# A streaming-encoder block in three-pass fp32: the second query block's mixed heads are loaded earlier, and two output-projection products take the last chunk last

## The chip, the cores and the metric

The kernel runs on one core of one Trainium2 chip. The metric is the device time of one execution in microseconds. An execution is somewhat longer than the span that the profiler shows from its first to its last instruction.

## The reference

One transformer-like layer over 2048 positions of width 1024, in float32:

```python
h = rms_norm(x, norm_mix_g)
z = h @ w_in                                   # columns: u_a, v_a (512 each), q, k, v (512 each), 8 forget logits
out_a = u_a * (masked W_s @ LN(v_a) + b)       # 8 gated-MLP heads, blocks of 128 positions
c = cumsum(log_sigmoid(f_logit))
s = q @ k.T / 8 + c[t] - c[s], causal          # 8 forgetting-attention heads of size 64
out_b = softmax(s) @ v
x = x + concat(out_a, out_b) @ w_out           # the output projection, 1024 x 1024
a = rms_norm(x, norm_ffn_g) @ w_up             # 1024 -> 2 x 2816
a = causal depthwise conv of width 3 over positions
x = x + (silu(g) * val) @ w_down
out = rms_norm(x, norm_final_g)
```

## The kernel before

**Arithmetic.** A float32 product is made of three passes: each operand is split into a high and a low part, and hi·hi, hi·lo and lo·hi are added in PSUM. `mm3` (L209) issues them: 8 chunks of 128 along the contracted dimension, three products each, 24 of 128x512 per output tile. `whi`/`wlo` are parts of weights (GpSimd makes `whi` at L152 from the loaded `raw`, VectorE `wlo`), `thi`/`tlo` parts of activations.

**Stages.** The 2048 rows are two halves of 1024, each half two blocks of 512 (`tb` = 0 to 3). The program first makes norms, `w_in` and the gated-MLP heads for all rows. `c_half(0)` is the output projection of the first half, `d_half` its up-projection with convolution, then the second half and the down-projection follow.

**Attention runs alongside.** It is a generator with many small steps. Each product of the dense stages calls `tick`, and after a certain number of products one step of attention is written into the program, with a priority that puts it some way ahead of the dense work around it. `need(tb)` writes steps until the heads of block `tb` are done. The flag `self.ready` lets the heads of the second half (`tb` of 2 and 3) begin. For each pair of heads, `b_max` looks for the row maxima (key products L829, VectorE reductions L832), `b_mix` computes scores (L877, L881), exponentials (L886), the high part `ph` and low part `pl` (L891, L892), their sum (L894) and the product with V (L865, L866). At the end of a pair both heads are put into one tile `op` (L906, L907), the reciprocal sums are turned by four transposes into `s` and multiplied in (L923). The pair is then split by `split_sb` (L203, L204) and written to DRAM, to `mixh` and `mixl`, from where the output projection loads it.

**The last pair of the first half** (`h` = 7, `tb` = 1) does not take the way through DRAM: it is split straight into chunk 7 of the projection's operand. `load_mix(1, given)` therefore loads only chunks 0 to 6, in pieces of two chunks. An operand has two tiles for each of hi and lo: one with chunks 0 to 3 and one with chunks 4 to 7.

**The output projection** (`c_half`) takes the two blocks `b` in turn, in each two column halves of `w_out` (in the order 0, 1 and then 1, 0, so that the weights of column half 1 are used twice in a row), in each four output tiles `t` of 128 rows. Such a tile is a PSUM sum "mm", of which there are two banks. VectorE adds the row of x to it (L971), and after the second column half the row is written to DRAM (`rows`), scaled by its norm (ScalarE L180, GpSimd L976, tile `ar`), and later transposed in pieces ("dn", L190) and split (L199, L200) for the up-projection.

**What sets the order.** The written order, the priorities and a scheduler that simulates the engines give the order on each engine; within an engine instructions run in that order. All loads and stores are issued by SyncE (SP) from line L102, in order. `issue_after(i)` keeps a load from being issued ahead of instruction `i`.

Of the kernel before, what the change touches and what calls it, by code (L numbers as in the profile page):

```python
# [8 lines left out]
F32 = mybir.dt.float32  # L9
# [9 lines left out]
P = 128  # L19
S = 2048  # L20
D = 1024
KC = D // P
# [3 lines left out]
TB = 512  # L26
# [7 lines left out]
AHEAD_B, AHEAD_W = 100, 2000  # L34
# [20 lines left out]
def f32(ap):  # L55
    return ap.bitcast(F32)
# [26 lines left out]
class Block:  # L83
# [51 lines left out]
    def start_fill(self, gen, rate):  # L135
        self.fill, self.rate, self.credit = gen, rate, 0.0

    def need(self, tb):

        while self.done < 8 * (tb + 1):  # L140
            self.step()
            self.count += 3
            while self.late and self.late[0][0] <= self.count:
                self.late.pop(0)[2]()
# [62 lines left out]

        self.split(self.transpose4(pp, tag, cols), g, hi, lo)

    def mm3(self, ps, ah, al, bh, bl, every=1):  # L210

        n = len(ah)
        for i in range(3 * n):
            k = i // 3
            a, b = ((ah, bh), (ah, bl), (al, bh))[i % 3]
            self.last_mm = self.nc.tensor.matmul(ps, lhsT=a[k], rhs=b[k], start=i == 0, stop=i == 3 * n - 1).ins  # L216
            if i % every == 0:
                self.tick()
# [635 lines left out]
    def b_mix(self, h, tb, t1, turn):  # L854

        nc, bp, pp = self.nc, self.bp, self.bpp
        t2 = self.b_low(h, tb)
        po = self.til(pp, [P, TB], F32, "o")
        total = self.room([P, TB], F32, "sum")
        ns = 4 * tb + 4  # L860
        late = []

        def pv():
            sc, c, v, ph, pl = late.pop(0)
            nc.tensor.matmul(po[:, c], lhsT=v, rhs=ph[:, c], start=sc == 0, stop=False)  # L865
            nc.tensor.matmul(po[:, c], lhsT=v, rhs=pl[:, c], start=False, stop=sc == ns - 1)  # L866

        for sc in range(ns):
            if sc == TURN and turn:
                turn()  # L870
            if sc % 4 == 0:
                m1, m2, v4 = self.b_keys(h, sc // 4, True)
            j = max(0, sc - 4 * tb)
            c = slice(j * P, TB)
            ks = slice((sc % 4) * P, (sc % 4 + 1) * P)
            ps = self.scores([P, TB])
            nc.tensor.matmul(ps[:, c], lhsT=m1[:, ks], rhs=t1[:, c], start=True, stop=False)  # L877
            if sc >= 4 * tb and not tb:
                nc.tensor.matmul(ps[:, j * P:(j + 1) * P], lhsT=self.same, rhs=self.maskT, start=False, stop=False,
                                 skip_group_check=True)  # L880
            nc.tensor.matmul(ps[:, c], lhsT=m2[:, ks], rhs=t2[:, c], start=False, stop=True)  # L881
            if sc >= 4 * tb and tb:
                d = ps[:, j * P:(j + 1) * P]
                nc.vector.tensor_tensor(d, d, self.maskT, op=ALU.add)
            e = self.room([P, TB], F32, "e") if sc else total
            nc.scalar.activation(e[:, c], ps[:, c], AF.Exp, scale=-1.0)  # L886
            if len(late) >= (LAG + 1 if self.more else LAG):
                pv()
            ph = self.room([P, TB], F32R, "ph")
            pl = self.room([P, TB], F32R, "pl")  # L890
            nc.scalar.activation(ph[:, c], e[:, c], AF.Copy)  # L891
            nc.vector.tensor_tensor(pl[:, c], e[:, c], f32(ph[:, c]), op=ALU.subtract)  # L892
            if sc:
                nc.vector.tensor_tensor(total[:, c], total[:, c], e[:, c], op=ALU.add)  # L894
            late.append((sc, c, v4[:, sc % 4, :], ph, pl))
            yield
        while late:
            pv()
            yield

        if h % 2 == 0:
            self.op = self.til(self.mp, [P, TB], F32, "op")
            self.fold = self.til(self.mp, [P, TB], F32, "rw")
        op, fold = self.op, self.fold
        own, other = (slice(0, 64), slice(64, 128)) if h % 2 == 0 else (slice(64, 128), slice(0, 64))
        nc.scalar.activation(op[own, :], po[other, :], AF.Copy)  # L906
        nc.vector.tensor_tensor(op[own, :], po[own, :], op[own, :], op=ALU.add)  # L907
        nc.scalar.activation(fold[own, :], total[other, :], AF.Copy)
        nc.vector.tensor_tensor(fold[own, :], fold[own, :], total[own, :], op=ALU.add)
        if h % 2 == 0:  # L910
            return

        yield
        ps = self.scores([P, 4, 2])
        for i in range(4):
            nc.tensor.matmul(ps[:, i, :], lhsT=fold[:, i * P:(i + 1) * P], rhs=self.pair, start=True, stop=True)
        rr = self.til(bp, [P, 4, 2], F32, "rr")
        nc.vector.reciprocal(rr, ps)
        rw = self.til(self.mp, [P, 4, 2, 64], F32, "rw")
        nc.scalar.activation(rw, rr.unsqueeze(3).broadcast_to([P, 4, 2, 64]), AF.Copy)  # L920
        yield
        pr = self.transpose4(None, "s", [rw[:, i, :, :].rearrange("p a b -> p (a b)") for i in range(4)])
        nc.vector.tensor_tensor(op, pr, op, op=ALU.mult)  # L923
        if h == 7 and tb == 1:
            self.mix1 = self.parts(1)
            self.split_sb(op, *[part[:, 7, :] for part in self.mix1])
            return
        oh = self.room([P, TB], F32R, "ph")
        ol = self.room([P, TB], F32R, "pl")
        self.split_sb(op, oh, ol)  # L930
        cs = slice(512 + (h - 1) * 64, 512 + (h + 1) * 64)
        self.dma(self.mixh[tb][cs, :], f32(oh))
        self.dma(self.mixl[tb][cs, :], f32(ol))
# [11 lines left out]
    def c_half(self, half, accp):  # L945
        nc, pp = self.nc, self.dpp
        mix = [self.mix0, None]
        for b in range(2):
            mh, ml = mix[b]
            rows, acc = [], []  # L950
            for t in range(4 * b, 4 * b + 4):
                x = self.til(accp, [P, D], F32, "acc")
                t0 = half * HALF + t * P
                acc_ins = self.dma(x, self.a["x"][0, t0:t0 + P, :]).ins
                acc.append(x)
            for col in (b, 1 - b):
                if b == 0 and col == 1:
                    self.need(2 * half + 1)
                    with self.tc.issue_after(acc_ins):
                        mix[1] = self.load_mix(1, self.mix1)  # L960
                cs = slice(col * 512, (col + 1) * 512)
                if b == 0 or col == 0:
                    us = [self.load_unit(self.a["w_out"][4 * col + j], 512) for j in range(4)]
                    wh = [us[k // 2][0][:, k % 2, :] for k in range(KC)]
                    wl = [us[k // 2][1][:, k % 2, :] for k in range(KC)]
                for t in range(4):
                    ts = slice(t * P, (t + 1) * P)
                    ps = self.til(pp, [P, TB], F32, "mm")
                    self.mm3(ps, [mh[:, k, ts] for k in range(KC)], [ml[:, k, ts] for k in range(KC)], wh, wl)
                    ac = acc[t]  # L970
                    nc.vector.tensor_tensor(ac[:, cs], ps, ac[:, cs], op=ALU.add)  # L971
                    if col == 1 - b:
                        self.dma(self.rows_d[half][4 * b + t], ac)
                        row = self.til(self.rowp, [P, D], F32, "ar")
                        r = self.row_scale(self.dp, ac, row)
                        nc.gpsimd.tensor_scalar(row, ac, r, 0.0, ALU.mult, ALU.add)  # L976
                        rows.append(row)
            hi, lo = self.hT[b] = self.parts(b)

            def turn(c, rows=rows, hi=hi, lo=lo):  # L980
                self.transpose_split(pp, "dn", [r[:, c * P:(c + 1) * P] for r in rows],
                                     self.g_ffn[:, c:c + 1], hi[:, c, :], lo[:, c, :])

            for c in range(KC):
                self.defer(26 + 8 * c, lambda c=c, turn=turn: turn(c))
# [574 lines left out]
    def run(self):  # L1560
# [16 lines left out]
        self.dp = dstack.enter_context(tc.tile_pool(name="dpool", bufs=1, reuse_waits="tile"))  # L1577
        self.accs, self.bxs = ExitStack(), ExitStack()
        self.rowp = self.accs.enter_context(tc.tile_pool(name="rowp", bufs=1, reuse_waits="tile"))
        self.ready = True  # L1580
        self.rate = RATES[2]
        self.c_half(0, accp)
        self.rate = RATES[3]
# [51 lines left out]
```

## Time and profile before

| | |
|---|---|
| runs | 2373.01, 2375.96, 2376.89 us (median 2375.96) |
| profiled execution | 2374.53 us, its span 2372.8 |
| mean granted TensorE clock | 0.998 |
| DMA | 374.29 MB, mean 158 GB/s |

The profile is of one execution. Its rows give starts and durations in microseconds from the start of the span. PE is TensorE, PEld its weight loads, DVE VectorE, ACT ScalarE, POOL GpSimd, SPq the issue of DMAs by SyncE. A number in brackets behind a row is the idle time of the engine ahead of it, and what ended it. Rows of a timeline group like instructions (x4), and the duration is that of the whole group. Ends of matmuls are modelled, so two neighbours may overlap in the rows.

### The profile page before, as it was taken

To read this page: it belongs to the slowest core of one execution; us is meant where nothing else is said; L and a number is where in the kernel's file an instruction comes from. 1 tells how busy PE (TensorE), PEld (TensorE's weight loads), DVE (VectorE), ACT (ScalarE), POOL (GpSimd) and SP (SyncE) were. 2 spreads that over 40 slices of the span, in tenths; PEclk is the share of its full clock that TensorE was granted. 3 is DMA by queue.
4 is the path that set the end of the run, shared out by engine and by line. 5 is a ranking of instruction groups with operands and counts; after the bars stand their busy time and mean duration, and the time that the engine had idled before them with its cause. 6 is when DMAs were issued, how large, how long until landed. Compare 5 with 4: busy or idle time off the path is not lost.

```text
span 2372.8 us, 32085 instructions
## 1 busy us (share of the span) xinstructions
PE 2348.2 (99%) x11144; PEld 1957.7 (83%) x11144; DVE 1883.7 (79%) x3146; ACT 1215.6 (51%) x2189; POOL 281.3 (12%) x278
## 2 busy tenths in 40 slices
PE   9999999999899999999999999999999999999998
PEld 7988888988787888888888888788888888888887
DVE  7458777876679888999899986698888887866875
ACT  4346646533436555656566654555545555454444
POOL 4114140100223111111100101100000000000001
PEclk9999999999999999999999999999999999999999
DMA  6763625568645444444444474222222238438633
GB/s 213 197 227 113 191 87 168 156 191 269 219 144 205 165 149 143 148 164 165 150 146 149 151 244 147 93 71 80 80 81 98 80 133 292 147 124 291 199 114 125
DMA packets 232818, 374.29 MB, mean 158 GB/s; under 512 B 49784, under 2 KB 109304, under 8 KB 231232
## 3 DMA queue, kind: packets, MB, share of 16 engines
q1 hardware_dynamic: 227616, 348.12, 45.5%
q0 software_dynamic: 5040, 24.12, 2.6%
q8 instruction: 88, 1.44, 0.2%
q14 instruction: 74, 0.61, 0.1%
HBM read 279.10 MB, written 93.20 MB: 157 GB/s over the span
## 4 chain that ended last, share of the span: by engine, by line
PE 91%; DVE 4%; DMA 2%; issue 1%; ACT 1%; POOL 1%; SPq 0%; POOLq 0%; DVEq 0%; ACTq 0%
PE mm L216 43%; PE D L1449 15%; PE A L1247 3%; PE A L1249 3%; PE A L1248 3%; PE o L866 3%; PE o L865 3%; PE s L881 2%; PE s L877 2%; PE s L829 2%; PE B L1248 2%; PE B L1249 2%; PE B L1247 2%; PE C L1247 1%; PE C L1248 1%
## 5 line engine op out<-in xcount | busy, mean ns | idle before, releaser
L216 PE MATMUL mm<-thi,whi 128*128 128x512 f32 x896 | 351.4, 392 | 1.2 <-DVE vn L538 1.2
L216 PE MATMUL mm<-thi,wlo 128*128 128x512 f32 x896 | 351.8, 393 | 0.0
L216 PE MATMUL mm<-tlo,whi 128*128 128x512 f32 x896 | 351.8, 393 | 0.0
L216 PE MATMUL mm<-whi,thi 128*128 128x512 f32 (+2 forms) x768 | 275.5, 359 | 6.4 <-DMA thi<-mixh 5.0
L216 PE MATMUL mm<-wlo,thi 128*128 128x512 f32 (+2 forms) x768 | 274.7, 358 | 0.0
L216 PE MATMUL mm<-whi,tlo 128*128 128x512 f32 (+2 forms) x768 | 273.7, 357 | 0.0
L216 PEld LDWEIGHTS mm<-thi,whi 128*128 128x128 f32 x896 | 168.6, 188 | 36.0 <-POOL whi L152 1.1
L216 PEld LDWEIGHTS mm<-tlo,whi 128*128 128x128 f32 x896 | 168.5, 188 | 34.5
L216 PEld LDWEIGHTS mm<-thi,wlo 128*128 128x128 f32 x896 | 168.6, 188 | 34.1
L216 PEld LDWEIGHTS mm<-whi,thi 128*128 128x128 f32 x768 | 144.9, 189 | 26.5 <-DMA thi<-mixh 5.3
L169 DVE TENSOR_TENSOR wlo<-raw,whi 128x1024 fp32r<-128x1024 f32 (+2 forms) x106 | 132.5, 1250 | 40.1 <-POOL whi L152 24.6
L216 PEld LDWEIGHTS mm<-wlo,thi 128*128 128x128 f32 x768 | 145.0, 189 | 19.3
L216 PEld LDWEIGHTS mm<-whi,tlo 128*128 128x128 f32 x768 | 144.6, 188 | 19.4
L886 ACT ACTIVATE e<-s 128x512 f32<-128x512 f32 (+3 forms) x204 | 104.0, 521 | 90.9 <-PE s L881 50.2
L1006 DVE SCALAR_TENSOR_TENSOR t<-a,cols,t 128x512 f32<-128x512 f32 (+2 forms) x176 | 139.4, 792 | 11.7 <-ACT t L1000 10.9
L1449 PE MATMUL D<-wl,xh 128*128 128x512 f32 x368 | 141.3, 389 | 0.0
L1449 PE MATMUL D<-wh,xh 128*128 128x512 f32 x368 | 140.8, 389 | 0.2 <-DVE xo L1550 0.2
L1449 PE MATMUL D<-wh,xl 128*128 128x512 f32 x368 | 137.5, 389 | 0.0
L152 POOL TENSOR_SCALAR whi<-raw 128x1024 fp32r<-128x1024 f32 (+3 forms) x70 | 79.9, 1144 | 484.7 <-PE mm L216 360.7
L894 DVE TENSOR_TENSOR sum<-sum,e 128x512 f32<-128x512 f32 (+3 forms) x189 | 119.5, 632 | 17.1 <-ACT e L886 15.7
L892 DVE TENSOR_TENSOR pl<-e,ph 128x512 fp32r<-128x512 f32 (+3 forms) x189 | 115.4, 616 | 12.5 <-PE o L866 10.6
L891 ACT ACTIVATE ph<-e 128x512 fp32r<-128x512 f32 (+3 forms) x189 | 101.8, 548 | 28.4 <-PE o L865 13.7
(1931 smaller groups left out, 5749.0 us busy)
## 6 DMA issues: line engine op xcount, KB each, us to landing
raw<-in_w_up_dram SPq DMA_DIRECT2D x72, 512.0 KB
x<-act SPq DMA_DIRECT2D x84, 256.0 KB
m<-kx SPq DMA_DIRECT2D x67, 256.0 KB
v<-vd SPq DMA_DIRECT2D x67, 256.0 KB
m<-kx SPq DMA_DIRECT2D x119, 136.0 KB
raw<-in_w_in_dram SPq DMA_DIRECT2D x28, 512.0 KB
raw<-in_w_out_dram SPq DMA_DIRECT2D x24, 512.0 KB
tw<-in_w_down_dram SPq DMA_DIRECT2D x11, 1024.0 KB
```

What stands on the lines that cost most here:

```text
L152: self.cast_ins = self.nc.gpsimd.tensor_scalar(out, in_, 1.0, 0.0, ALU.mult, ALU.add).ins
L169: nc.vector.tensor_tensor(lo, raw, f32(hi), op=ALU.subtract)
L216: self.last_mm = self.nc.tensor.matmul(ps, lhsT=a[k], rhs=b[k], start=i == 0, stop=i == 3 * n - 1).ins
L886: nc.scalar.activation(e[:, c], ps[:, c], AF.Exp, scale=-1.0)
L891: nc.scalar.activation(ph[:, c], e[:, c], AF.Copy)
L892: nc.vector.tensor_tensor(pl[:, c], e[:, c], f32(ph[:, c]), op=ALU.subtract)
L894: nc.vector.tensor_tensor(total[:, c], total[:, c], e[:, c], op=ALU.add)
L1006: nc.vector.scalar_tensor_tensor(t[:, c], a[:, n + c.start:n + TB], cw[:, cc], t[:, c], op0=ALU.mult, op1=ALU.add)
L1247: mm(ps, lhsT=xh[:, ks], rhs=yh[:, k, :], start=fresh and k == 0, stop=False, **kw)
L1248: mm(ps, lhsT=xh[:, ks], rhs=yl[:, k, :], start=False, stop=False, **kw)
L1249: mm(ps, lhsT=xl[:, ks], rhs=yh[:, k, :], start=False, stop=k == 3, **kw)
L1449: nc.tensor.matmul(bank[t], lhsT=x[i][:, ts], rhs=w[k], start=fresh and j == 0 and i + k == 0, stop=last and i == 1, **kw)
```

## The change

`need` can stop some steps early. In the first block of `c_half`, right behind the loads of x, the operand of the second block is allocated and its chunks 0 to 6 are loaded. The split of the last pair is kept back as a function and called at the second column half of block 0, with the priority of attention; then `self.ready` is set, which was set ahead of `c_half` before. In block 1, the column half that comes first there computes chunks 0 to 6 of its first two output tiles, and then chunk 7 of the one and of the other.

```diff
-    def need(self, tb):
+    def need(self, tb, left=0):
-        while self.done < 8 * (tb + 1):
+        while self.done < 8 * (tb + 1) - left:
...
-    def mm3(self, ps, ah, al, bh, bl, every=1):
+    def mm3(self, ps, ah, al, bh, bl, every=1, first=0, end=KC):
         n = len(ah)
-        for i in range(3 * n):
+        for i in range(3 * first, 3 * min(end, n)):
...
         if h == 7 and tb == 1:
-            self.mix1 = self.parts(1)
-            self.split_sb(op, *[part[:, 7, :] for part in self.mix1])
+            self.last_pair = lambda parts: self.split_sb(op, *[part[:, 7, :] for part in parts])
             return
...
+            if not b:
+                self.need(1, 2)
+                with self.tc.issue_after(acc_ins):
+                    mix[1] = self.load_mix(1, self.parts(1))
             for col in (b, 1 - b):
                 if b == 0 and col == 1:
-                    self.need(2 * half + 1)
-                    with self.tc.issue_after(acc_ins):
-                        mix[1] = self.load_mix(1, self.mix1)
+                    self.need(1)
+                    with self.tc.high_priority(AHEAD_B):
+                        self.last_pair(mix[1])
+                    self.ready = True
...
+                sums = {}
+
+                def chunks(t, first, end):
+                    ts = slice(t * P, (t + 1) * P)
+                    if t not in sums:
+                        sums[t] = self.til(pp, [P, TB], F32, "mm")
+                    self.mm3(sums[t], [mh[:, k, ts] for k in range(KC)], [ml[:, k, ts] for k in range(KC)], wh, wl,
+                             first=first, end=end)
+
                 for t in range(4):
-                    ts = slice(t * P, (t + 1) * P)
-                    ps = self.til(pp, [P, TB], F32, "mm")
-                    self.mm3(ps, [mh[:, k, ts] for k in range(KC)], [ml[:, k, ts] for k in range(KC)], wh, wl)
+                    if b == col == 1 and t == 0:
+                        chunks(0, 0, KC - 1)
+                        chunks(1, 0, KC - 1)
+                    chunks(t, KC - 1 if b == col == 1 and t < 2 else 0, KC)
+                    ps = sums[t]
...
-        self.ready = True
         self.rate = RATES[2]
         self.c_half(0, accp)
```

How the order of instructions moves. On SP, behind the four loads of x for block 0 (`acc`), the kernel before has the loads of chunks 4 to 6 of the second block's operand, then keys of attention (`m`):

```order
L102 DMA acc_6338<-in_x_dram 128x1024
L102 DMA thi_5558<-mixh_82 128x2x512
L102 DMA tlo_5560<-mixl_86 128x2x512
L102 DMA thi_5558<-mixh_82 128x512
L102 DMA tlo_5560<-mixl_86 128x512
L102 DMA m_49_422<-kx_75 68x512
```

Some 30 places further on it has those of chunks 0 to 3 (`thi_5557` and `tlo_5559`), behind loads of x for block 1 and stores of finished rows of block 0:

```order
L102 DMA acc_6942<-in_x_dram 128x1024
L102 DMA v_6696<-vd_79 128x4x128
L102 DMA rows_3_92<-acc_6338 128x1024
L102 DMA thi_5557<-mixh_82 128x2x512 x2
L102 DMA m_49_422<-kx_76 68x512
L102 DMA tlo_5559<-mixl_86 128x2x512 x2
```

In the changed kernel, the same first place of SP:

```order
L102 DMA acc_6332<-in_x_dram 128x1024
L102 DMA thi_6334<-mixh_82 128x2x512
L102 DMA tlo_6336<-mixl_86 128x2x512
L102 DMA thi_6334<-mixh_82 128x2x512
L102 DMA tlo_6336<-mixl_86 128x2x512
L102 DMA thi_6335<-mixh_82 128x2x512
L102 DMA tlo_6337<-mixl_86 128x2x512
L102 DMA thi_6335<-mixh_82 128x512
L102 DMA tlo_6337<-mixl_86 128x512
L102 DMA m_49_422<-kx_75 68x512
```

The four loads of chunks 0 to 3 have moved ahead of those of chunks 4 to 6, to the place behind the x loads. On TensorE, around the last pair's transposes (`s_5551`), the kernel before has the end of the first block (`mm_6870`), transposes of its finished rows, keys of the next heads, and then the second block's first products (`mm_6946`, `mm_6988`):

```order
L190 MATMUL s_5551<-ident,rw_5541 128x128 x4
L829 MATMUL s_6371<-m_49_422,t_51_424 128x512
L829 MATMUL s_6379<-m_49_422,t_51_424 128x512
L829 MATMUL s_6386<-m_49_422,t_51_424 128x512
L829 MATMUL s_6394<-m_49_422,t_51_424 128x512
L829 MATMUL s_6402<-m_48_421,t_51_424 128x512
L190 MATMUL dn_6991<-ident,ar_6926 128x128
L190 MATMUL dn_7031<-ident,ar_6926 128x128
L829 MATMUL s_6409<-m_48_421,t_51_424 128x512
L829 MATMUL s_6419<-m_48_421,t_51_424 128x512
L216 MATMUL mm_6946<-whi_6563,thi_5557 128x512
L216 MATMUL mm_6946<-wlo_6564,thi_5557 128x512
```

In the changed kernel, 18 products of the second block's first sum (`mm_6738`, chunks 0 to 5) stand ahead of these rows, which hold the same transposes:

```order
L216 MATMUL mm_6738<-whi_6495,thi_6335 128x512
L216 MATMUL mm_6738<-wlo_6496,thi_6335 128x512
L190 MATMUL s_5551<-ident,rw_5541 128x128 x4
L829 MATMUL s_6508<-m_49_422,t_51_424 128x512
L829 MATMUL s_6516<-m_49_422,t_51_424 128x512
L216 MATMUL mm_6738<-whi_6495,tlo_6337 128x512
L216 MATMUL mm_6798<-whi_6477,thi_6334 128x512
L216 MATMUL mm_6798<-wlo_6478,thi_6334 128x512
```

Further on, the two sums end with chunk 7, whose operands come from the last pair (the last six rows, behind chunk 6 of `mm_6798`):

```order
L216 MATMUL mm_6798<-whi_6495,thi_6335 128x512
L216 MATMUL mm_6798<-wlo_6496,thi_6335 128x512
L216 MATMUL mm_6798<-whi_6495,tlo_6337 128x512
L216 MATMUL mm_6738<-whi_6495,thi_6335 128x512
L216 MATMUL mm_6738<-wlo_6496,thi_6335 128x512
L216 MATMUL mm_6738<-whi_6495,tlo_6337 128x512
L216 MATMUL mm_6798<-whi_6495,thi_6335 128x512
L216 MATMUL mm_6798<-wlo_6496,thi_6335 128x512
L216 MATMUL mm_6798<-whi_6495,tlo_6337 128x512
```

Between the last pair's transposes and its chunk there now stand 22 products of the second block, where before the block's first product stood behind everything shown.

## The prediction

> **What bounds the kernel now.** I read the engines' shares first, then the chain of work that ended last.
>
> ```profile
> PE 2348.2 (99%) x11144; PEld 1957.7 (83%) x11144; DVE 1883.7 (79%) x3146; ACT 1215.6 (51%) x2189; POOL 281.3 (12%) x278
> ...
> PE 91%; DVE 4%; DMA 2%; issue 1%; ACT 1%; POOL 1%; SPq 0%; POOLq 0%; DVEq 0%; ACTq 0%
> ```
>
> TensorE is the bound nearly everywhere. The change adds no product and removes none, so it can gain only where TensorE stands still or runs slowly. The table of its waits has one large entry, which is in the place that the change edits:
>
> ```profile
> PE mm L216 <- DMA thi<-mixh: 5.0, 1, 5.0
> ```
>
> The stretches around that wait, ten microseconds each and four inside it (columns: busy time and instructions of TensorE, its weight loads, VectorE, ScalarE, GpSimd; then granted clock, DMA share, GB/s), and the chain of waits through it:
>
> ```profile
> 630.00:640.00 10.00, 8.06 (x42) 5.57 (x41) 6.58 (x13) 4.27 (x7) 3.55 (x5) 1.00 0.62 186
> 640.00:650.00 10.00, 5.87 (x23) 4.99 (x24) 5.13 (x11) 1.38 (x2) 0.00 (x0) 0.66 0.92 329
> 642.00:646.00 4.00, 1.87 (x4) 1.49 (x5) 0.28 (x1) 0.00 (x0) 0.00 (x0) 0.50 1.07 365
> ```
>
> ```profile
> 636.08 0.70 DVE op L923
> ...
> 636.78 0.36 SPq L102
> ...
> 637.20 6.89 DMA thi<-mixh
> ```
>
> The second block's first product needs the mixed heads of chunks 0 to 3, and that transfer is issued at 637.20 and lands 6.89 us later. Behind the wait the clock is at 0.50 for a while. TensorE's own timeline shows what both cost:
>
> ```profile
> 633.08 0.27 PE L866 MATMUL o<-pl,v 128*128 128x128 f32 x1
> ...
> 633.71 0.82 PE L190 MATMUL dn<-ident,ar 128*128 128x128 f32 x6
> 634.37 0.60 PE L190 MATMUL s<-ident,rw 128*128 128x128 f32 x4
> ...
> 644.13 0.79 PE L216 MATMUL mm<-whi,thi 128*128 128x512 f32 x1 [5.01 <-DMA thi<-mixh]
> 644.72 0.63 PE L216 MATMUL mm<-wlo,thi 128*128 128x512 f32 x1
> 645.15 0.63 PE L216 MATMUL mm<-whi,thi 128*128 128x512 f32 x1
> ...
> 648.12 0.48 PE L216 MATMUL mm<-whi,tlo 128*128 128x512 f32 x1
> 648.44 0.40 PE L216 MATMUL mm<-whi,thi 128*128 128x512 f32 x1
> 648.67 0.39 PE L216 MATMUL mm<-wlo,thi 128*128 128x512 f32 x1
> ...
> 651.35 0.60 PE L190 MATMUL dn<-ident,ar 128*128 128x128 f32 x4
> 651.71 0.48 PE L216 MATMUL mm<-whi,tlo 128*128 128x512 f32 x1
> ```
>
> Starts tell the true pace, since ends are modelled: 0.23 us from one 512-column product to the next (648.44 to 648.67), 0.43 at the half clock (644.72 to 645.15), 0.09 for a transpose (0.36 for the four at 651.35).
>
> **What the stall costs.** From the first block's last product (the next start is 633.71) to the first product at full pace (648.44) pass 14.73 us. In them stand 20 transposes at 0.09 (1.8), eight key products L829 of 512 columns at 0.23 (1.8), two narrow ones (0.2) and five products L216 at 0.23 (1.2): 5.0 us of work. So 14.73 − 5.0 = **9.7 us are lost** here. A lower bound is from the windows: idle 1.94 + 4.13 = 6.1, and half of 644.13 to 648.12 for the slow clock, 2.0, together 8.1; the busy column hides the rest, because modelled ends of slow products reach into idle time. I take 9.7, counted from starts.
>
> On the slow clock: the 2.0 us is read from the rows, four slow microseconds of which two are lost. The Trainium skill, "TensorE: Matmul & The Clock Gate", Part 1, says that an idle window of about 3.4 us drops the clock to half and about 3.4 us of sustained work restores it; the 5.01 us wait and the 0.50 agree, and by its 3.4 us the loss would be 1.7 and the sum 0.3 smaller. By the same rule a remaining wait well under 3.4 us would keep the full clock; no row here shows that.
>
> **The change, part by part.**
>
> *Loads of chunks 0 to 6 early.* Before, the loads of chunks 4 to 6 already stand right behind the four x loads, and those of chunks 0 to 3 about 50 us later, behind writes of finished rows. The DMA queue's own rows:
>
> ```profile
> 585.51 0.43 SPq L102 DMA_DIRECT2D thi<-mixh  x1
> 585.99 1.34 SPq L102 DMA_DIRECT2D tlo<-mixl  x1
> 587.37 0.67 SPq L102 DMA_DIRECT2D thi<-mixh  x1
> 588.08 0.57 SPq L102 DMA_DIRECT2D tlo<-mixl  x1
> 592.32 7.71 SPq L102 DMA_DIRECT2D m<-kx  x3
> ...
> 602.59 9.78 SPq L102 DMA_DIRECT2D raw<-in_w_out_dram  x4
> ```
>
> In the order of the changed kernel all eight stand together there, so the data is in place some 40 us ahead of its use and the 5.01 us wait goes whole, with the slow clock behind it. The cost: four more issues, 3.0 us by the four rows above (0.43 + 1.34 + 0.67 + 0.57), in a gap from 588.65 to 592.32 of 3.7; and four transfers of 512 KB, 2.1 MB, which at the 404 GB/s of the third window below last 5.2 us:
>
> ```profile
> 582.00:586.00 4.00, 4.00 (x19) 3.31 (x18) 1.44 (x7) 0.00 (x0) 0.00 (x0) 1.00 0.84 244
> 586.00:590.00 4.00, 4.00 (x19) 3.15 (x18) 1.29 (x2) 2.72 (x5) 0.00 (x0) 1.00 0.85 289
> 590.00:594.00 4.00, 4.00 (x20) 3.22 (x19) 3.81 (x7) 1.17 (x3) 0.00 (x0) 1.00 1.03 404
> 594.00:598.00 4.00, 4.00 (x21) 3.40 (x20) 3.28 (x8) 1.46 (x3) 0.00 (x0) 1.00 0.62 230
> 598.00:602.00 4.00, 4.00 (x20) 3.35 (x19) 3.63 (x6) 1.55 (x4) 2.42 (x2) 1.00 0.21 37
> 602.00:606.00 4.00, 4.00 (x19) 3.33 (x18) 3.90 (x6) 1.64 (x4) 0.65 (x1) 1.00 0.97 310
> ```
>
> The free DMA share from 582 to 602 is 0.64 + 0.60 + 0 + 1.52 + 3.16 = 5.9 us. It just fits ahead of the weight loads at 602.59. Between 0 (hidden) and 5.2 (all of it late) I take 0, since TensorE is 4.00 of 4.00 busy in every one of these windows, so nothing there is late today. From 637 to 644 the same 2.1 MB disappear from the queue.
>
> *The last pair split later, its chunk last.* The split waits for the last pair's product with V, a transpose and a multiply, so chunk 7 is the only piece that comes this late. Its chain before:
>
> ```profile
> 633.39 0.59 ACT L906 ACTIVATE op<-o 64x512 f32<-64x512 f32 x1 [0.58 <-PE o L866]
> 636.81 0.63 ACT L203 ACTIVATE thi<-op 128x512 fp32r<-128x512 f32 x1 [1.02 <-DVE op L923]
> ```
>
> ```profile
> 634.63 0.69 DVE L907 TENSOR_TENSOR op<-o,op 64x512 f32<-64x512 f32 x1
> 636.08 0.69 DVE L923 TENSOR_TENSOR op<-s,op 128x512 f32<-128x512 f32 x1
> 638.48 0.68 DVE L204 TENSOR_TENSOR tlo<-op,thi 128x512 fp32r<-128x512 f32 x1
> ```
>
> From the start of the pair's transposes (634.37) to the end of the high part (636.81 + 0.63) pass 3.1 us, to the end of the low part (638.48 + 0.68) 4.8. In the new order 20 products of the second block (4.6 us) stand between the last V product and these transposes, and behind them, up to the first use of chunk 7, 22 products, five L829 and eight transposes: 27 × 0.23 + 8 × 0.09 = 6.9 us, with the pair's four 7.3. The margin is 4.2 us for the high part and, two products further on, 3.0 for the low part. So the products of chunks 0 to 6 cover the chain: cost 0. As both PSUM banks for these sums stay open until chunk 7 is in, the third sum waits for the residual add of the first; the three products of the second sum's chunk 7 (0.7 us) stand in between and an add takes 0.7, so 0 to 0.7; I take **0.5**. The short waits of the old place (0.67 and 0.32 us for VectorE at 636) are within the 9.7, and go because products of chunks 0 to 6 now stand there.
>
> *The later heads released later.* The second half's attention is let in when the last pair is split, some 96 products later in the program. In the new order up to 47 of its TensorE instructions are behind their old place, against the dense products (near 890 us), and 1 is by the 145th dense group (near 990 us). It is the same work, later. TensorE has dense products to run instead. VectorE is what could run short, in the part where the lag is made up:
>
> ```profile
> 1000.00:1340.00 340.00, 340.00 (x1551) 281.48 (x1550) 319.17 (x563) 206.62 (x414) 41.36 (x35) 1.00 0.47 156
> ```
>
> It is busy 319 of 340 there with TensorE still 340 of 340, so 20.8 us are free. The cost lies between a small gain (less VectorE work while the first half's rows are normalised) and the 14.7 us of rival B; I take 0, because almost all of the lag is paid back ahead of 1000 us.
>
> **Sum.** 2374.53 (this execution: span 2372.8 and 1.73 around it) − 9.7 + 0.5 = 2365.3. The median of the runs, 2375.96, lies 1.43 above this execution, so **2366.8**. Its own range: the fastest run shown is 2.95 under the median, hence 2363.5 below; above, with a saving of 8.1 instead of 9.7 and some of the 5.2, about 2369.
>
> **Rivals.**
>
> A. *The early loads crowd the weights.* For: the fit is close (5.2 into 5.9, 3.0 into 3.7), the w_out loads already need 9.78 us for four, and GpSimd waits for them. Against: TensorE does not wait for these weights now. If all 5.2 us arrive at TensorE: 2366.8 + 5.2 = 2372.0. The Trainium skill, "DMA: Bandwidth & Descriptors", section "Queues, rings and completion order", says that each DMA engine takes its descriptors in ring order, so what is issued early runs ahead of the weights; the share 1.03 at 590 to 594 fits that, and no run yet shows what it does to the weights. Chance 0.12.
>
> B. *The other side: the lag is not paid back.* If 47 instructions, about 12 pieces of four instructions, still lag when VectorE is full, each brings a subtraction and a sum at the end:
>
> ```profile
> L894 DVE TENSOR_TENSOR sum<-sum,e 128x512 f32<-128x512 f32 (+3 forms) x189 | 119.5, 632 | 17.1 <-ACT e L886 15.7
> L892 DVE TENSOR_TENSOR pl<-e,ph 128x512 fp32r<-128x512 f32 (+3 forms) x189 | 115.4, 616 | 12.5 <-PE o L866 10.6
> ```
>
> 47 / 4 × (0.632 + 0.616) = 14.7 us. Then 2366.8 + 14.7 = 2381.5. It decides against the change once more than 9.2 us of it stay, that is when over 29 of the 47 still lag at 1000 us; the order says 1, and 20.8 us are free. Chance 0.06.
>
> C. *The wait moves to chunk 7.* If ScalarE or VectorE run the split late, both open sums wait, up to the pair's whole chain: 4.8 us, 2371.6. For: nothing else can run in the meantime. Against: margins of 4.2 and 3.0. Chance 0.05.
>
> D. *The loads do not come early after all*, held in the queue by an earlier wait: 2376.0. Against: chunks 4 to 6 are issued from that place today without one. Chance 0.05.
>
> **Chances.** My forecast has 0.72. A measurement of this kernel tells 0.2%, 4.75 us, from no change: faster is below 2371.2. The forecast is there, and partial cases of A and C (0.07); same are D, half of B's partial outcomes and the full forms of A and C (0.15); slower is B (0.06). The range 2363.5 to 2372.5 holds the forecast and the full A and C, and leaves out B, D and a larger gain than counted.
>
> **What would show it.** Right: no wait for thi<-mixh on TensorE, a clock of 1.00 in the windows where 0.66 stood, eight loads in a row behind the x loads, and about 9 us less at the start of the up-projection. A would show TensorE waiting for whi near 610 us, C a wait for L203 or L204 ahead of a chunk 7 product, B equal time up to about 1000 us and new VectorE waits behind it, D the old rows. Wrong would be the forecast if the stretch shrinks by 9.7 us but the end doesn't.

## The result and the profile after

The changed kernel takes 2361.51 us (median of six runs, 2360.25 to 2362.57) where the kernel before takes 2375.47 (six runs): a ratio of 0.9939, with an interval of 0.9929 to 0.9950, that is 14.0 us less. Two more comparisons on other occasions gave 0.9948 (0.9934 to 0.9961) and 0.9943 (0.9930 to 0.9955), 12.4 and 14.3 us. Forecast were 9.2 us, and a time between 2363.5 and 2372.5: the direction was right, the gain half as large again as forecast. The experiments show besides that the forecast's reason was only half of the story.

The profiled execution took 2360.25 us, its span 2358.5. Its engines, and the table of TensorE's waits:

```profile
PE 2343.5 (99%) x11144; PEld 1956.8 (83%) x11144; DVE 1877.2 (80%) x3146; ACT 1212.3 (51%) x2189; POOL 283.3 (12%) x278
```

```profile
PE tp L292 <- POOL ident masks.py:199: 1.5, 1, 1.5
PE mm L216 <- DVE fs L536: 1.4, 1, 1.4
PE tq L190 <- DVE cv L1114: 1.3, 1, 1.3
PE mm L216 <- DVE acc L986: 0.7, 1, 0.7
```

The entry for `thi<-mixh`, 5.0 us before, is gone, and so is the 1.3 us for GpSimd's `ar`. The two stretches around the old wait (columns as in the prediction's windows):

```profile
630.00:640.00 10.00, 10.00 (x56) 8.45 (x55) 4.08 (x7) 3.33 (x6) 1.85 (x3) 1.00 0.66 212
640.00:650.00 10.00, 10.00 (x52) 8.25 (x51) 7.80 (x12) 2.42 (x4) 0.00 (x0) 1.00 0.40 130
```

TensorE is busy throughout, at full clock. The loads stand where the order said (the DMA queue's issues):

```profile
583.90 0.44 SPq L102 DMA_DIRECT2D thi<-mixh  x1
...
590.28 0.41 SPq L102 DMA_DIRECT2D tlo<-mixl  x1
591.60 6.72 SPq L102 DMA_DIRECT2D m<-kx  x3
...
600.88 11.65 SPq L102 DMA_DIRECT2D raw<-in_w_out_dram  x4
```

And the last pair's split is done in time on ScalarE and VectorE, behind the transposes at 636.52:

```profile
637.88 0.63 ACT L203 ACTIVATE thi<-op 128x512 fp32r<-128x512 f32 x1 [4.01 <-DVE op L923]
```

```profile
638.96 0.68 DVE L204 TENSOR_TENSOR tlo<-op,thi 128x512 fp32r<-128x512 f32 x1
```

**Where the time went.** I added up, over each stretch, the distance from one TensorE start to the next beyond the usual distance of its kind (the lower quartile of that kind in the same trace). Two profiles of the kernel before and three of the changed kernel give, in us:

| stretch | before | after |
|---|---|---|
| 0 to 580 (the same order in both) | 30.4, 28.9 | 28.0, 31.6, 27.6 |
| 634 to 650 | 10.2, 9.5 | 1.2, 1.3, 1.2 |
| 700 to 750 | 4.4, 5.4 | 2.2, 2.2, 2.2 |
| all the rest | 30.0, 31.7 | 29.8, 29.2, 30.5 |
| sum | 75.0, 75.5 | 61.2, 64.3, 61.4 |

The forecast's place gave 8.6 us on average, the one at 700 to 750 another 2.7, which the forecast doesn't have. The rest is about as large as what executions of the same order differ by.

The second place is the end of the second block. Before, the last row of that block is scaled on GpSimd behind the weights of the up-projection (L152), whose load it waits for, and TensorE's transposes wait for this row (GpSimd's and TensorE's timelines):

```profile
709.63 1.05 POOL L152 TENSOR_SCALAR whi<-raw 128x1024 fp32r<-128x1024 f32 x1 [6.60 <-DMA raw<-in_w_up_dram]
...
712.73 1.12 POOL L976 TENSOR_SCALAR ar<-acc,rstd 128x1024 f32<-128x1024 f32 x1
```

```profile
713.90 0.33 PE L190 MATMUL dn<-ident,ar 128*128 128x128 f32 x1 [1.34 <-POOL ar L976]
```

After, GpSimd scales that row at 691.26, and no such wait is left:

```profile
691.26 1.69 POOL L991 TENSOR_SCALAR ar<-acc,rstd 128x1024 f32<-128x1024 f32 x1
```

### The profile page after: what moved, and what is told of

It reads as the page before. It is cut to its first block, busy times and chain, and to the rows that moved or that the text cites. A ratio compares the mean times of both kernels' runs of the same rounds, so it can differ in the third digit from the quotient of the medians.

```text
span 2358.5 us, 32076 instructions
## 1 busy us (share of the span) xinstructions
PE 2343.5 (99%) x11144; PEld 1956.8 (83%) x11144; DVE 1877.2 (80%) x3146; ACT 1212.3 (51%) x2189; POOL 283.3 (12%) x278
## 4 chain that ended last, share of the span: by engine, by line
PE 91%; DVE 4%; DMA 2%; issue 1%; ACT 1%; POOL 0%; SPq 0%; POOLq 0%; DVEq 0%; ACTq 0%
PE mm L216 44%; PE D L1464 12%; PE A L1262 3%; PE A L1263 3%; PE A L1264 3%; PE o L866 3%; PE o L865 3%; PE s L881 2%; PE s L829 2%; PE s L877 2%; PE B L1263 2%; PE B L1264 2%; PE B L1262 2%; DMA x<-act 1%; PE C L1262 1%
## 5 line engine op out<-in xcount | busy, mean ns | idle before, releaser
L152 POOL TENSOR_SCALAR whi<-raw 128x1024 fp32r<-128x1024 f32 (+3 forms) x70 | 80.0, 1144 | 477.9 <-PE mm L216 339.7
```

The lines of the kernel that those rows point to most:

```text
L152: self.cast_ins = self.nc.gpsimd.tensor_scalar(out, in_, 1.0, 0.0, ALU.mult, ALU.add).ins
```

## The experiments

All counts of dense products below are counts in the order of instructions: 128x512 products of `mm3` on TensorE ahead of a place. A ratio is to the kernel before, run on the same occasion, with a 95% interval in brackets.

**The loads alone, the release alone, all but the release, and the kernel before again.** The theories: P, the gain is that of the first place; R, what the forecast missed comes from the later release of the second half's heads; V, it is variation.

```diff
 # e1_loads_alone: the kernel before with the split kept back as in the change, and in block 0 ahead of the column halves
+                self.need(1, 2)
+                with self.tc.issue_after(acc_ins):
+                    mix[1] = self.load_mix(1, self.parts(1))
+                with self.tc.high_priority(AHEAD_B):
+                    self.last_pair(mix[1])
...
 # e2_release_alone: the kernel before with, at the second column half of block 0,
+                    self.ready = True
...
 # and ahead of c_half without
-        self.ready = True
...
 # e3_all_but_release: the changed kernel, with self.ready = True ahead of c_half again
```

> The kernel before with one part of the change: the second block's operand is taken and its chunks 0 to 6 are loaded behind the x loads, the last pair is split right there in the program; the output projection's products stay in the written order of chunks, and the later heads are released ahead of c_half as before. Theory P (the place): the early loads take away the 5.0 us wait and the half clock, so the saving is 9 to 10 us against the kernel before, and about 4 us of the change's 14.0 are missing: 2365 to 2367. Theory R (release): the same, as the 4 to 5 us that my forecast missed come from the later heads' release, which is not in this kernel. Theory V (variation): the missing part is not a matter of the order at all, and this kernel shows some 12 to 14 us, 2361 to 2363. In the trace P and R leave the stall near 700 to 715 us for GpSimd's ar.

Measured: 2376.37 us, ratio 1.0001 (0.9992 to 1.0010). No gain at all. (The loads, and the split of the last pair that moves with them, were not taken apart; the two together are called the early loads below.)

> The kernel before, with the later heads released where the change does it (at the second column half of block 0) and nothing else. Theory R: the stall for GpSimd's ar near 713 us goes (1.3 to 2.2 us) with one or two us more behind it, so 2 to 5 us faster than before, 2371 to 2373; the 5.0 us wait for thi<-mixh stays. Theory P or V: same as before within 2 us. Rival B of my forecast (a lag that is not paid back) would make it slower by up to 14.7 us.

Measured: 2373.92 us, ratio 0.9991 (0.9983 to 1.0000). At most a small gain, as theories P and V said; the waits for `thi<-mixh` (4.7 us) and for `ar` (1.6) are both still there, against theory R.

> The changed kernel with the later heads released ahead of c_half, as before. Theory R: it loses the 4 to 5 us that my forecast missed, 2365 to 2367. Theory V: as the changed kernel, 2360 to 2363. In the trace R brings the wait for ar back near 700 us.

Measured: 2376.61 us, ratio 1.0002 (0.9993 to 1.0011). None of the three theories said so.

> The kernel before once more, for a second profile of it and for what a comparison of this size shows when nothing differs: ratio 1.000 within 0.001. Theory V: the two stalls at 408.8 (1.8 us) and 464.9 (0.9 us) of the first profile and the 1.07 us at 2274 are not there again, or have other sizes. If the whole program before 580 us, which is the same in both kernels, is systematically slower in the kernel before, they are there again with the same sizes.

Measured: 2375.71 us, ratio 1.0000 (0.9991 to 1.0010). The wait of 1.6 us for `ph` at 410 us, in the first profile of the kernel before, is 0.4 us here; in the profiles of this study it has between nothing and 1.7 us, the changed kernel's included.

In the kernel with the loads alone the first place is as good as in the changed kernel:

```profile
630.00:640.00 10.00, 10.00 (x55) 8.43 (x54) 4.08 (x7) 3.40 (x6) 1.85 (x3) 1.00 0.75 205
640.00:650.00 10.00, 10.00 (x52) 8.29 (x51) 7.72 (x12) 2.34 (x4) 0.00 (x0) 1.00 0.32 111
```

So the 9 us are won there, and given back. Where, the waits of "all but the release" say, and its chain of work through that wait, 830 us later:

```profile
PE mm L216 <- DMA thi<-mixh: 7.1, 1, 7.1
```

```profile
1467.79 0.45 PE s L190 x4
1468.27 0.70 DVE op L923
1468.99 0.64 ACT ph+_3176_13680 L203
1469.65 1.98 DMA mixh<-ph+_3176_13680
1471.69 3.58 DMA thi<-mixh
1475.31 4.61 PE mm L216 x12
```

It is the same kind of wait in the second half's output projection: the last pair of heads of block 3 goes through DRAM there (written in 1.98 us, read back in 3.58), and TensorE has nothing else left to do. In the kernel before this place had no wait. The stretch from 1455 to 1485 us, first of the kernel before, then of "all but the release":

```profile
1455.00:1485.00 30.00, 30.00 (x149) 25.18 (x149) 12.16 (x22) 11.97 (x18) 3.60 (x8) 1.00 0.59 210
```

```profile
1455.00:1485.00 30.00, 22.48 (x105) 18.42 (x104) 12.89 (x24) 13.26 (x22) 3.48 (x8) 0.89 0.42 153
```

7.5 us idle, and a slow clock behind it. Added up from starts as above, "all but the release" wins about 8.5 us at 634 to 650 and 2.7 at 700 to 750, and loses about 9.5 at 1455 to 1500 and 1.8 at 1500 to 1600, so that nothing is left of the gain. The order shows why. With the early loads the attention of the second half falls back against the dense products, by 78 to 80 of them at its first head and by 63 to 80 at its last V product. With the late release it comes forward by about 100 again, at one place: head 4 of block 2. Its mixing steps run interleaved with the row maxima of head 5 when the late release is there, and one after the other when it isn't, since the second set of buffers that allows it (`self.more`) is opened at a fixed place of the program.

| V products, at dense product | before | loads alone | release alone | all but release | changed |
|---|---|---|---|---|---|
| block 2, head 0, first | 1724 | 1802 | 1724 | 1804 | 1804 |
| block 2, head 3, first | 2279 | 2351 | 2279 | 2380 | 2380 |
| block 2, head 4, first | 2502 | 2574 | 2401 | 2598 | 2499 |
| block 3, head 7, last | 4027 | 4090 | 3937 | 4107 | 4014 |

That gave theory S: the loads' gain is kept only if the second half's last pair is early enough.

**Moving the last pair by other means.**

```diff
 # e6_written_chunk_order: the changed kernel without the chunk order
-                    if b == col == 1 and t == 0:
+                    if False:
...
-                    chunks(t, KC - 1 if b == col == 1 and t < 2 else 0, KC)
+                    chunks(t, 0, KC)
 # e7_late_release_one_head_plain: the changed kernel, with
-            if todo and (self.more or tb == 0):
+            if todo and (self.more or tb == 0) and (h, tb) != (5, 2):
 # e8_early_release_head_held: all but the release, with
+            if (h, tb) == (5, 2):
+                while not self.more:
+                    yield
```

> The changed kernel once more, for a second profile and more runs: 2360 to 2363. Theory S (slack at the second half's last pair): no wait for thi<-mixh near 1460 to 1475 us, as in its first profile. Theory P (only the first place counts) says nothing else. The stall at 586 us for VectorE's m (0.86 us) should be there or not as in the other kernels, by chance, if the early loads have no part in it.

Measured: 2363.78 us, ratio 0.9948 (0.9934 to 0.9961), no wait for `thi<-mixh`, and none near 586 us.

> All but the release (the kernel that showed 2376.6), but head 5 of block 2 is held until the second set of buffers is open, so that it and all behind it run interleaved as in the changed kernel. The later heads are still released early. The last V product moves from dense product 4107 to 4060, 10.8 us earlier. Theory S (the early loads are paid back where the second half's last pair is late, and anything that brings this pair earlier keeps the gain): the 7.1 us wait near 1475 us shrinks below 2 us, and the time falls to 2362 to 2367. Theory R (it is the late release at the first place that counts): the time stays at 2375 to 2378, as the release is not moved.

Measured: 2365.37 us, ratio 0.9959 (0.9946 to 0.9973). The release is early as in "all but the release", and with the ratio going from 1.0002 to 0.9959 some 10 us are back. What is left of the wait, on TensorE:

```profile
1466.03 0.50 PE L216 MATMUL mm<-whi,thi 128*128 128x512 f32 x1 [1.25 <-DMA thi<-mixh]
...
1467.99 0.50 PE L216 MATMUL mm<-whi,tlo 128*128 128x512 f32 x1 [0.76 <-DMA tlo<-mixl]
```

> The changed kernel, but the first pair of heads that the late release lets run interleaved (row maxima of the next head between the mixing steps of this one: head 5 of block 2) runs one after the other, as in the kernel before. The last V product of the second half comes 34 dense products later than in the changed kernel (4048 against 4014), 7.8 us at 0.23. Theory S: the last pair's way through DRAM still just comes in time or is late by little, a wait of 0 to 3 us near 1465 us, 2361 to 2366. Theory P: no difference, 2360 to 2363.

Measured: 2366.24 us, ratio 0.9958 (0.9943 to 0.9973), 2.5 us slower than the changed kernel on the same occasion; TensorE is idle for 1.9 of the 30 us at 1455 to 1485, 1.1 of them for the last pair's two loads (0.58 and 0.56). S and R part in this run and the one told before it: the release counts through the last pair's place, not by itself. The interleaving of this one head is 34 of the 93 products that the release is worth at the last V product; the other 59, with the row maxima of head 5 written behind the opening of the second buffers, were not taken apart.

> The changed kernel without the output projection's edit: the first two products of the second block are written with chunk 7 in its place, loads and release as in the change. In the order of instructions the scheduler itself sets the first sum's chunk 7 behind most of the second sum, so theory S expects the changed kernel's time, 2360 to 2364, with the last V product of the second half 23 dense products later than in the changed kernel (4037 against 4014) and still in time. Theory C (the chunk order is what makes the early loads pay): the wait moves to chunk 7 at 637 us and some 3 to 5 us are lost, 2365 to 2367.

Measured: 2366.79 us, ratio 0.9960 (0.9947 to 0.9974), 3.0 us slower than the changed kernel on the same occasion, though the two intervals overlap. The time lies in theory C's range, but not for its reason: there is no wait at 637 us and none for `thi<-mixh` at 1470, so the scheduler's own order covers chunk 7 as well. The loss lies elsewhere, 1.0 us at 700 to 750 and 3.1 at 1500 to 1600, where TensorE waits 1.8 us for ScalarE's `t2h` and has the half clock for 3.4 us behind it. That wait is also there in the loads alone, with the head held or not, and in all but the release, and in no run of the changed kernel; why, I did not find out.

**Late without the loads, and early with the loads alone.**

```diff
 # e9_loads_alone_head_held: the loads alone, with head 5 of block 2 held as above
 # e10_before_last_pair_late: the kernel before, with
-            if todo and (self.more or tb == 0):
+            if todo and (self.more or tb == 0) and not (tb == 2 or (tb == 3 and h < 1)):
 # e11_change_more_slack: the changed kernel, with
+            if (h, tb) == (4, 2):
+                while not self.more:
+                    yield
```

> The kernel with the early loads alone (2376.4, no gain), plus head 5 of block 2 held until the second set of buffers is open. Products in the written order of chunks, early release. The last V product of the second half moves from dense product 4090 to 4037, 12.2 us earlier at 0.23. Theory S: below some 4040 there is no wait for the last pair near 1470 us, so the 6.8 us wait and the half clock behind it go: 2364 to 2368. Theory R (only the late release at the first place, or the chunk order, makes the loads pay): 2375 to 2378.

Measured: 2367.82 us, ratio 0.9964 (0.9952 to 0.9977), and the wait for `thi<-mixh` is gone. The loads alone, worth nothing, are worth 8.5 us once one head is interleaved. The release is early here and the chunks are in the written order, so neither is what makes the loads pay.

> The kernel before without any part of the change, but the last three pairs' halves of block 2 and the first head of block 3 run one after the other and not interleaved, which moves the last V product of the second half from dense product 4027 to 4074. Theory S: the lateness itself costs, with or without early loads; between the kernels at 4060 and 4090 the stretch from 1455 to 1485 lost 3 to 7 us of TensorE, so a wait for thi<-mixh appears near 1480 us and the kernel is 4 to 9 us slower than before, 2379 to 2385. If the loss at 1470 us came from the early loads themselves and not from the lateness of the last pair: no wait there, 2374 to 2378.

Measured: 2380.95 us, ratio 1.0023 (1.0013 to 1.0033): 4.6 us slower than before. The table of waits now has two for `thi<-mixh`, the old one and one at the second half's place, which the timeline shows with its clock (windows: the column ahead of the last two):

```profile
PE mm L216 <- DMA thi<-mixh: 8.2, 2, 5.3
```

```profile
1481.94 0.80 PE L216 MATMUL mm<-whi,thi 128*128 128x512 f32 x1 [2.83 <-DMA thi<-mixh]
1482.53 0.63 PE L216 MATMUL mm<-wlo,thi 128*128 128x512 f32 x1
1482.96 0.63 PE L216 MATMUL mm<-whi,thi 128*128 128x512 f32 x1
```

```profile
1480.00:1482.00 2.00, 0.06 (x1) 0.07 (x1) 0.00 (x0) 2.00 (x4) 1.16 (x3) 0.93 0.97 368
1482.00:1484.00 2.00, 2.00 (x5) 1.49 (x6) 0.00 (x0) 2.00 (x3) 0.00 (x0) 0.50 0.99 318
```

So a late last pair costs without the early loads too.

> The changed kernel with the last pair still earlier: head 4 of block 2 is held until the second set of buffers is open, and the last V product moves from dense product 4014 to 3961. Theory S says that slack beyond what covers the pair's way through DRAM is worth nothing: the same as the changed kernel on this chip within 1.5 us, 2360 to 2364. If a late last pair still cost something spread out, it would be 2 us or more faster.

Measured: 2364.14 us, ratio 0.9949 (0.9937 to 0.9962).

> The changed kernel on the same chip as the three others, for the comparison with the kernel that has more slack: 2360 to 2364, no wait near 1470 us.

Measured: 2361.97 us, ratio 0.9943 (0.9930 to 0.9955). More slack (last V product at 3961 instead of 4014) brings nothing, as S says; the 2.2 us between the two are more than the 1.5 expected, but their intervals do not tell them apart. No version here beats the changed kernel.

All kernels by the place of the last V product (busy time of TensorE in the 30 us from 1455 to 1485, from the windows, and its waits there for the last pair's loads):

| kernel | last V product | TensorE busy | waits for the last pair | time |
|---|---|---|---|---|
| release alone | 3937 | 30.00 | 0 | 2373.92 (no early loads) |
| more slack | 3961 | 30.00 | 0 | 2364.14 |
| changed | 4014 | 30.00 | 0 | 2361.51, 2363.78, 2361.97 |
| before | 4027 | 30.00 | 0 | 2375.47 (no early loads) |
| written chunk order | 4037 | 30.00 | 0 | 2366.79 |
| loads alone, head held | 4037 | 29.16 | 0 | 2367.82 |
| one head plain | 4048 | 28.08 | 1.1 | 2366.24 |
| head held, early release | 4060 | 27.21 | 2.0 | 2365.37 |
| before, last pair late | 4074 | 27.17 | 2.8 | 2380.95 (no early loads) |
| loads alone | 4090 | 23.19 | 6.8 | 2376.37 |
| all but release | 4107 | 22.48 | 7.1 | 2376.61 |

Up to 4037 the pair's way through DRAM is covered; from 4048 on there is a wait, and it is the longer the later the pair comes, though not in proportion. The rest of the idle time has other causes, such as 0.84 us for VectorE's `acc` in the loads alone with the head held. The kernel before stood 10 products, 2.3 us, ahead of the last place that was still covered. Its trace agrees: the pair's two loads land 3.0 and 2.1 us ahead of the first products on them (1476.21 for 1479.17, 1478.78 for 1480.87). In the changed kernel it is 3.6 and 3.8 us.

## Why the prediction was right and where it was wrong

**The stall's size** was right: 9.7 us forecast for the first place, 9.0 in the first pair of profiles (10.2 to 1.2) and 8.6 on average.

**The loads' cost** of 0 was right for that stretch, though not for the program (see below). They were issued in the gap (591.60 for the next keys, 592.32 before) and the four weight loads took 11.65 us of issue instead of 9.78, but TensorE waits for none of them. Rival A did not come.

**The cover of chunk 7** was right. Transposes at 636.52, high part done at 638.51 and low part at 639.64; TensorE does not wait for either. The 0.5 us for the third sum's wait for a PSUM bank did not come: no TensorE wait shows from 600 to 700 us. Rival C did not come, and the run with the written order shows that the products' edit was not needed for it. What that edit is worth lies elsewhere, the 3.0 us by which that run is slower.

**The step that failed in the sum** is that it has only one place where TensorE gains. The second block's end, 700 to 750 us, brings 2.7 us more. Its wait of 1.3 us for `ar` was in the table of waits, but the change touches nothing there by name, and I left it out. It went with the loads, not with the release: "release alone" still has 1.6 us of it, "all but the release" none. The lower end of the range, 2363.5, allowed for the spread of the runs and for no gain beyond the one counted. With this term the forecast would have been 2364.1, 2.6 us above the measured 2361.5. The bank's 0.5 us that did not come and a kernel before that is 0.5 us faster in six runs than in three (2375.47) go one way, and a place that gave 1.1 us less than 9.7 goes the other. What remains lies in small parts over the span, none of them larger than what executions of one order differ by; its cause stays open.

**The step that failed in the mechanism** is *The later heads released later*, with its cost of 0. I saw the lag of the second half's heads and its recovery by 990 us, put the lag down to the release, and read the recovery as a cost avoided. The runs show the opposite signs. The release alone leaves the first head of block 2 where it was (1724) and brings the last V product forward by 90 dense products. It is the early loads that put the first head back, by 78 to 80. The 47 instructions that I counted as a lag compared the changed kernel with the one before, two opposite shifts already added up.

So two terms of the sum that stood at 0 are not 0. By themselves the early loads put the last pair of the second half 63 to 80 products back, over an edge of which the kernel before was some 10 products short. The wait comes back there, longer than the old one (6.8 and 7.1 us against 5.0), and all of the gain is lost (2376.37 for the loads alone, 2376.61 with the products' edit). The release, taken as neutral, wins it back: the second of these kernels takes 2361.51 with it. That these two nearly cancel, so that the forecast came near and its direction was right, was luck: nothing in my reasoning looked at the last pair at 1470 us. Rival B, a lag that is not paid back, is the nearest to what I should have asked, but it put the price on VectorE's work at 1000 to 1340 us and not on that place, where the same kind of wait could arise.

**The clock.** I wrote that by the Trainium skill ("TensorE: Matmul & The Clock Gate", Part 1) a wait well under 3.4 us would keep the full clock. A wait of 1.25 us kept it; one of 2.83 us did not: 0.50 from 1482 to 1484 in the run above. Waits of 1.6 to 1.8 us did both, as the last section shows.

## What to carry to other kernels

When a wait is taken out of one stage and another chain runs beside that stage at its own pace, look for the next place where the two meet, and count how much cover is left there: a saving may only move to it. Take apart an edit that seems neutral beside the main one; here the loads alone gave 0.0%, the release alone 0.1%, both together 0.4%, and with the products' order 0.5 to 0.6%. And compare orders part by part, since the total difference of two versions can be the sum of two opposite shifts.

## What was not expected of the hardware

An idle time of 2.83 us was enough to halve the granted clock: it fell to 0.93 in the last two of the idle microseconds and stood at 0.50 behind them, and products came 0.43 us apart from 1482.53 to 1482.96. Two idle times of 1.25 and 0.76 us, 2 us apart, left it at 1.00.

Between these the size of the wait does not decide. TensorE waited 1.64 to 1.71 us for `ph` near 411 us in three executions (first profile of the kernel before, second of the changed kernel, one head plain), and the clock stayed at 1.00. In the kernel with more slack it waited 1.74 us there, and the clock was halved. The slow stretch began only about 1.7 us after the products had resumed, so it is easily missed when looking right behind a wait:

```profile
412.54 0.44 PE L868 MATMUL o<-ph,v 128*128 128x384 f32 x1 [1.74 <-ACT ph L894]
```

```profile
412.00:414.00 2.00, 1.46 (x10) 1.31 (x10) 2.00 (x7) 1.32 (x5) 0.00 (x0) 1.00 0.64 153
414.00:416.00 2.00, 2.00 (x10) 1.96 (x10) 1.61 (x5) 1.30 (x3) 0.00 (x0) 0.56 0.82 229
```

The wait for `t2h`, 1.78 to 1.79 us and 0.5 us shortly ahead of it, left the clock at 1.00 in all but the release. It halved it in the loads alone, with the head held or not, and in the kernel with the written chunk order, for 3.4 us each time. So such a wait cost 1.7 us more in some executions than in others.
